# Weight sums of a Winograd feed-forward product: formed by adding transfers instead of by VectorE

## The chip, the cores and the metric

The kernel runs on one core of one Trainium2 chip. The metric is the device time of one execution in microseconds (us); lower is better. Names used below: PE is the matrix engine (TensorE), DVE is VectorE, ACT is ScalarE, POOL is GpSimd, SP is the engine that issues the ordinary transfers.

## The reference, cut to what matters

One encoder block in float32 over 1024 tokens of width 1024: two gated branches (linear attention and windowed attention), an output projection, and a SwiGLU feed-forward layer. The change lies in the first feed-forward product:

```python
h2 = _rms_norm(x, norm_ffn_g[l])
gu = h2 @ w_ffn_in[l]                      # 1024 x 1024 times 1024 x 5632
ff_gate, ff_up = gu[..., :D_FF], gu[..., D_FF:]     # D_FF = 2816 = 22 tiles of 128
x = x + (jax.nn.silu(ff_gate) * ff_up) @ w_ffn_out[l]
```

## The kernel before, in words

Each float32 operand is split into a rounded high part and a low remainder (`wsplit` for weights, L853: ACT writes `wh`, then DVE writes `wl`), and each product is three passes (high-high, high-low, low-high). A `product` (L878) of four 128-row pieces is therefore 12 matmuls of 128x128 by 128x512.

The first feed-forward product uses the Winograd form of Strassen's scheme. For each of the 22 feature tiles f the weights are four blocks of 128x512: A11 and A12 (gate feature tile f, first and second half of the contraction), A21 and A22 (up feature tile f). The activations are four blocks B11, B12, B21, B22 (contraction half by token half), whose own combinations (`combos`, L720) are made once: T1, T2, T3, T4. Seven products per tile replace eight:

- `p11(f)`: A11 with B11, `p21(f)`: A12 with B21 added in the same bank. These give the gate of the first token half.
- `ffn_in(f)`: s1 with T1 (into the bank Z), s2 with T2 (into X), then the products named in `between`, then s3 with T3 (into X), s4 with B22 (into Z), A22 with T4 (into X). Here s1 = A21 + A22, s2 = s1 - A11, s3 = A11 - A21, s4 = A12 - s2, each formed by DVE in `comb` (L873, the addition is L875).

Below, "product 22(f)" is s4 with B22, "T3(f)" is s3 with T3, and so on. Between T2(f) and T3(f) stand one product for f = 0 to 5 (so a tile is six products there) and two for f = 6 to 20 (seven products).

The order of PE is that of the code (a manual schedule for PE alone). The order of DVE, ACT, SP and POOL is chosen by the framework's scheduler when the program is built, and each of these engines then runs its own list strictly in that order: an instruction that waits holds everything behind it. What an instruction waits for are semaphores; in the order shown below, DMASW0 to DMASW7 belong to transfers issued by POOL, DMAHW0 to DMAHW7 to those issued by SP.

Buffers that matter: `wh` and `wl` have five buffers each, so the split of a product can be made when the product five places earlier has ended; `ws` (the sums) has four, `wr` four, `wr2` three. Two reads of the banks free them: `u2` is read from X after T2(f) and before T3(f) overwrites it with its sum, and `c22` is read between T3(f) and A22 with T4. So T3(f) on PE waits for the DVE instruction that makes `u2` (L952 before, L955 after the change).

Of the kernel before, what the change touches and what calls it, by code (L numbers as in the profile page):

```python
# [12 lines left out]
ALU = mybir.AluOpType  # L13
# [8 lines left out]
NFF = 22  # L22
NA = 4
NB = 7
# [5 lines left out]
def body(tc, i, out):  # L30
    nc = tc.nc
    with ExitStack() as root:
# [8 lines left out]
        def nm(s):  # L41
            uid[0] += 1
            return f"{s}_{uid[0]}"

        def mmtile(shape=(P, 512), dt=F32):
            return psm.tile(list(shape), dt, tag="mm", name=nm("mm"))

        def chtile(shape, dt=F32):
            return psc.tile(list(shape), dt, tag="ch", name=nm("ch"))
# [634 lines left out]
        for n in range(2 * KT):  # L684
            g, t = divmod(n, KT)
# [25 lines left out]
        YX = {q: [] for q in ("11", "T1", "T2", "21", "22", "T3", "T4")}  # L711

        def bsplit(pool, tag, src):
            h = pool.tile([P, HT], FR, tag=tag + "h", name=nm(tag + "h"))
            l = pool.tile([P, HT], FR, tag=tag + "l", name=nm(tag + "l"))
            nc.scalar.activation(h, src, AF.Copy)
            nc.vector.tensor_tensor(l, src, h.bitcast(F32), op=ALU.subtract)
            return h, l

        def combos(k, step):  # L720

            b11, b12, b21, b22 = xg[k][0], xg[k][1], xg[k + 4][0], xg[k + 4][1]
            if step == 0:
                YX["11"].append(bsplit(big1, f"b11{k}", b11))
                YX["21"].append(bsplit(big1, f"b21{k}", b21))
            elif step == 1:
                nc.vector.tensor_tensor(b12, b12, b11, op=ALU.subtract)
                YX["T1"].append(bsplit(big2, f"bt1{k}", b12))
                YX["22"].append(bsplit(big2, f"b22{k}", b22))
                nc.vector.tensor_tensor(b22, b22, b12, op=ALU.subtract)  # L730
                YX["T2"].append(bsplit(big2, f"bt2{k}", b22))
                nc.vector.tensor_tensor(b11, b22, b11, op=ALU.subtract)
                nc.vector.tensor_tensor(b21, b21, b22, op=ALU.subtract)
            else:
                YX["T3"].append(bsplit(big3, f"bt3{k}", b11))
                YX["T4"].append(bsplit(big3, f"bt4{k}", b21))
# [116 lines left out]
        def wsplit(src, n):  # L853
            h = wp.tile([P, n], FR, tag="wh", name=nm("wh"), bufs=5)
            l = wp.tile([P, n], FR, tag="wl", name=nm("wl"), bufs=5)
            nc.scalar.activation(h, src, AF.Copy)  # L856
            nc.vector.tensor_tensor(l, src, h.bitcast(F32), op=ALU.subtract)  # L857
            return h, l

        def rload(f, q):  # L860

            if q < 20:
                u = i["w_fi"][f, q - 11]
            else:
                u = i["w_fi"][NFF + f, q - 21]
            if q % 10 == 1:
                t = wp.tile([P, 512], F32, tag="wr", name=nm("wr"), bufs=4)
            else:
                t = wq.tile([P, 512], F32, tag="wr2", name=nm("wr2"), bufs=3)
            nc.sync.dma_start(out=t, in_=u)  # L870
            return t

        def comb(x, y, op):  # L873
            t = wq.tile([P, 512], F32, tag="ws", name=nm("ws"), bufs=4)
            nc.vector.tensor_tensor(t, x, y, op=op)  # L875
            return t

        def product(o, w, x, nk, start, stop):  # L878
            h, l = w
            for kk in range(nk):  # L880
                c = slice(kk * P, (kk + 1) * P)
                nc.tensor.matmul(o, h[:, c], x[kk][0], start=start and kk == 0, stop=False, skip_group_check=True)  # L882
                nc.tensor.matmul(o, h[:, c], x[kk][1], start=False, stop=False, skip_group_check=True)  # L883
                nc.tensor.matmul(o, l[:, c], x[kk][0], start=False, stop=kk == nk - 1, skip_group_check=True)  # L884
# [9 lines left out]
        def ctile(tag):  # L894
            t = x1s.tile([P, HT], F32, tag="xg" + home[tag][turn[tag] % len(home[tag])], name=nm(tag))
            turn[tag] += 1
            return t
# [12 lines left out]
        def put(q, j, k, t):  # L910
            d = scratch(f"{q}{j}_{k}")
            nc.sync.dma_start(out=d, in_=t)
            scr[q, j, k] = d
# [5 lines left out]
        def p11(f):  # L919
            F = feats[f]  # L920
            F.Y = mmtile()
            if f < NB:
                w = wunit(i["w_fi"][f, 0])
            else:
                F.r11 = rload(f, 11)
                w = wsplit(F.r11, 512)
            product(F.Y, w, YX["11"], 4, True, False)
            F.p1 = ctile("a" if f < NA else "p1")
            nc.scalar.copy(F.p1, F.Y)
# [6 lines left out]

        def ffn_in(f, between):
            F = feats[f]
            if f < NB:
                F.r11 = rload(f, 11)  # L940
            F.r12, F.r21, F.r22 = (rload(f, q) for q in (12, 21, 22))
            p1 = F.p1
            Z, X = chtile((P, HT)), mmtile()
            s1 = comb(F.r21, F.r22, ALU.add)
            product(Z, wsplit(s1, 512), YX["T1"], 4, True, False)
            p5 = ctile("p5")
            nc.scalar.copy(p5, Z)
            nc.vector.tensor_tensor(p5, p5, p1, op=ALU.add)
            s2 = comb(s1, F.r11, ALU.subtract)
            product(X, wsplit(s2, 512), YX["T2"], 4, True, False)  # L950
            u2 = ctile("u2")
            nc.vector.tensor_tensor(u2, X, p1, op=ALU.add)  # L952
            for p, g in between:
                p(g)
            s3 = comb(F.r11, F.r21, ALU.subtract)  # L955
            product(X, wsplit(s3, 512), YX["T3"], 4, False, False)
            c22 = ctile("c22")
            nc.vector.tensor_tensor(c22, X, p5, op=ALU.add)
            s4 = comb(F.r12, s2, ALU.subtract)
            product(Z, wsplit(s4, 512), YX["22"], 4, False, True)  # L960
            nc.vector.tensor_tensor(u2, Z, u2, op=ALU.add)
            nc.vector.tensor_tensor(u2, u2, r1, op=ALU.mult)
            nc.scalar.activation(u2, u2, AF.Silu)
            nc.vector.tensor_tensor(u2, u2, r1, op=ALU.mult)
            product(X, wsplit(F.r22, 512), YX["T4"], 4, False, True)
            c21, g0 = ctile("c21"), F.g0
            nc.vector.tensor_tensor(c21, X, p1, op=ALU.add)
            nc.vector.tensor_tensor(c21, c21, g0, op=ALU.mult)
            nc.vector.tensor_tensor(c22, c22, u2, op=ALU.mult)
            put("B1" if f < DK else "B2", 1, f % DK, c21)  # L970
            put("B1" if f < DK else "B2", 2, f % DK, c22)

            if f < DK:
                t1 = hp.tile([P, HT], F32, tag="tx", name=nm("tx"), bufs=4)
                nc.vector.tensor_tensor(t1, c22, c21, op=ALU.subtract)
                put("T", 1, f, t1)
            else:
                b12, t1, t4 = (hp.tile([P, HT], F32, tag="tx", name=nm("tx"), bufs=4) for _ in range(3))
                nc.sync.dma_start(out=b12, in_=scr["B1", 2, f - DK])
                nc.sync.dma_start(out=t1, in_=scr["T", 1, f - DK])  # L980

                def tsum(j, d, x, y):
                    nc.vector.tensor_tensor(d, x, y, op=ALU.subtract)
                    put("T", j, f - DK, d)

                for v in ((2, t1, c22, t1), (3, b12, c22, b12), (4, t4, c21, t1)):
                    if f < NFF - 1:
                        tsum(*v)
                    else:
                        later.append(lambda v=v: tsum(*v))  # L990
# [61 lines left out]
        with tc.manual_schedule(engines={mybir.EngineType.PE}):  # L1052
            for k in range(4):
                combos(k, 0)
# [10 lines left out]
            for k in range(4):  # L1065
                combos(k, 2)
# [5 lines left out]
            for f in range(NFF):  # L1072
                ffn_in(f, between.get(f, [(p21, f), (p11, f + 1)]))
# [11 lines left out]
            def banks(f):  # L1085
                return [f() for _ in range(4)]
# [14 lines left out]
            Z, X = banks(mmtile), banks(lambda: chtile((P, HT)))  # L1101
            fo_product(Z, 11, ("B1", 1), True, True, lambda k: aload(fo1, 11, k), nop, (fo2, 12), (fo2, 21))
            p1 = [ctile("o1") for _ in range(4)]
# [8 lines left out]
            Z = banks(mmtile)  # L1112
            fo_product(Z, 22, ("T", 4), True, True, lambda k: aload(fo3, 22, k), step4)
            c21 = [ctile("o4") for _ in range(4)]
            add4(c21, Z, p1)
            residual4(c21, 1, 0)
            X = banks(lambda: chtile((P, HT)))
# [4 lines left out]
            Z = banks(mmtile)  # L1122
# [89 lines left out]
```

## Time and profile before

| | |
|---|---|
| median of 3 runs | 1688.89 us (1688.65 to 1688.97) |
| span of the profiled execution | 1687.4 us (the median is 1.5 us above it: the time around the first and last instruction) |
| PE / DVE / ACT / POOL busy | 1670.9 / 1181.0 / 869.3 / 0.2 us |
| first feed-forward product | about 1049 to 1469 us of the span, 22 tiles |
| traffic | 245.85 MB in transfers, mean 146 GB/s, all of it issued by SP |

A row of groups reads: line, engine, operation, output<-input, shapes, count, then the busy time in us, the mean of one in ns, and the idle time before it with what ended it. A row of the timeline reads: start, duration, engine, line, operation, output<-input.

### The profile page before, as it was taken

The numbers are of one execution on the slowest core, as the hardware profiler recorded it, in microseconds if no ns is written. First come the engines' busy times: TensorE is split into PE (matmuls) and PEld (weight loads), VectorE is DVE, ScalarE is ACT, GpSimd is POOL, SyncE is SP. The second block draws the span as 40 slices with busy tenths as digits, with TensorE's granted clock in tenths as the row PEclk, the third lists the DMA queues.
The fourth block names the chain that finished last, engine by engine and source line by source line (L and its number), as shares of the span: only waits on it lengthen the run. The fifth ranks groups of instructions, "written<-read, shape, count | busy, mean of one in ns | idle before, by whom it ended". The sixth has DMA issues, their size and how long they took to land.

```text
span 1687.4 us, 23673 instructions
## 1 busy us (share of the span) xinstructions
PE 1670.9 (99%) x7880; PEld 1390.1 (82%) x7880; DVE 1181.0 (70%) x2454; ACT 869.3 (52%) x1939; POOL 0.2 (0%) x4
## 2 busy tenths in 40 slices
PE   8999999999999999999999999999999999999999
PEld 6788888888788888888888888888888888788887
DVE  7767777764578666546674468987778877779755
ACT  7554767776557656544553466533333333354443
POOL 0000000000000000000000000000000000000000
PEclk9999999999999999999999999999999999999999
DMA  6533434444533233247764645344224443496433
GB/s 197 157 113 109 123 126 140 131 141 125 175 121 118 83 100 96 74 150 245 235 213 146 188 129 187 113 134 134 94 88 156 163 143 132 152 333 200 146 100 119
DMA packets 153738, 245.85 MB, mean 146 GB/s; under 512 B 17582, under 2 KB 43054, under 8 KB 153616
## 3 DMA queue, kind: packets, MB, share of 16 engines
q1 hardware_dynamic: 153616, 244.34, 45.6%
q8 instruction: 62, 1.02, 0.3%
q14 instruction: 60, 0.49, 0.1%
HBM read 177.17 MB, written 67.11 MB: 145 GB/s over the span
## 4 chain that ended last, share of the span: by engine, by line
PE 97%; DVE 2%; ACT 1%; DMA 0%; issue 0%; SPq 0%; ACTq 0%; DVEq 0%
PE mm L72 48%; PE ch L72 9%; PE mm L1029 7%; PE mm L884 6%; PE mm L882 6%; PE mm L883 6%; PE ch L1029 5%; PE ch L884 2%; PE ch L882 2%; PE ch L883 2%; PE ch L664 1%; PE ch L490 0%; PE ch L614 0%; PE ch L405 0%; DVE cs L364 0%
## 5 line engine op out<-in xcount | busy, mean ns | idle before, releaser
L66 ACT ACTIVATE wh<-wr 128x512 fp32r<-128x512 f32 (+1 forms) x256 | 160.1, 628 | 173.6 <-PE mm L72 149.5
L68 DVE TENSOR_TENSOR wl<-wr,wh 128x512 fp32r<-128x512 f32 (+1 forms) x256 | 174.9, 687 | 89.0 <-ACT wh L66 82.2
L72 PE MATMUL mm<-xh,wh 128*128 128x512 f32 x512 | 203.3, 397 | 5.9 <-ACT wh L66 5.9
L72 PE MATMUL mm<-xl,wh 128*128 128x512 f32 x512 | 203.4, 397 | 0.0
L72 PE MATMUL mm<-xh,wl 128*128 128x512 f32 x512 | 169.4, 397 | 0.0
L72 PE MATMUL mm<-wh,xh 128*128 128x512 f32 x320 | 126.7, 396 | 1.9 <-DVE st L146 1.2
L72 PE MATMUL mm<-wl,xh 128*128 128x512 f32 x320 | 127.3, 398 | 0.0
L72 PE MATMUL mm<-wh,xl 128*128 128x512 f32 x320 | 126.4, 395 | 0.0
L72 PEld LDWEIGHTS mm<-xh,wh 128*128 128x128 f32 x512 | 96.7, 189 | 22.4 <-ACT wh L66 5.9
L856 ACT ACTIVATE wh<-ws 128x512 fp32r<-128x512 f32 x88 | 55.7, 634 | 115.2 <-PE mm L883 69.3
L72 PEld LDWEIGHTS mm<-xl,wh 128*128 128x128 f32 x512 | 96.7, 189 | 16.9
L72 PEld LDWEIGHTS mm<-xh,wl 128*128 128x128 f32 x512 | 94.9, 189 | 16.7 <-DVE wl L68 0.2
L856 ACT ACTIVATE wh<-a 128x512 fp32r<-128x512 f32 x66 | 41.9, 635 | 90.9 <-PE ch L1029 42.2
L856 ACT ACTIVATE wh<-wr 128x512 fp32r<-128x512 f32 x52 | 33.0, 635 | 91.1 <-issue 49.5
L857 DVE TENSOR_TENSOR wl<-a,wh 128x512 fp32r<-128x512 f32 x66 | 45.5, 690 | 41.8 <-ACT wh L856 41.6
L72 PEld LDWEIGHTS mm<-wh,xh 128*128 128x128 f32 x320 | 60.2, 188 | 14.0 <-DVE st L146 1.6
L1029 PE MATMUL mm<-hh,wh 128*128 128x512 f32 x176 | 69.3, 394 | 1.6 <-ACT hh L1001 1.6
L1029 PE MATMUL mm<-hl,wh 128*128 128x512 f32 x176 | 69.1, 393 | 0.5 <-DVE hl L1002 0.5
L1029 PE MATMUL mm<-hh,wl 128*128 128x512 f32 x176 | 69.2, 393 | 0.1
L647 ACT ACTIVATE p<-p,nm,rs 128x384 f32<-128x384 f32 (+1 forms) x64 | 42.9, 673 | 50.3 <-DVE nm L641 50.3
L72 PEld LDWEIGHTS mm<-wh,xl 128*128 128x128 f32 x320 | 60.2, 188 | 10.4
L857 DVE TENSOR_TENSOR wl<-ws,wh 128x512 fp32r<-128x512 f32 x88 | 60.3, 685 | 11.9 <-ACT wh L856 11.9
(508 smaller groups left out, 4419.8 us busy)
## 6 DMA issues: line engine op xcount, KB each, us to landing
wr<-in_w_fi_dram SPq DMA_DIRECT2D x102, 256.0 KB, 2.9
wr<-in_w_t_dram SPq DMA_DIRECT2D x80, 256.0 KB, 2.8
wr<-in_w_f_dram SPq DMA_DIRECT2D x64, 256.0 KB, 2.7
B<-c SPq DMA_DIRECT2D x44, 256.0 KB, 2.1
T<-tx SPq DMA_DIRECT2D x44, 256.0 KB, 2.4
a<-in_w_fo_dram SPq DMA_DIRECT2D x44, 256.0 KB, 5.3
hr<-T SPq DMA_DIRECT2D x44, 256.0 KB, 2.7
hr<-B SPq DMA_DIRECT2D x33, 256.0 KB, 4.3
```

Of the source, the lines that this page charges most:

```text
L66: nc.scalar.activation(h, raw, AF.Copy)
L68: nc.vector.tensor_tensor(l, raw, h.bitcast(F32), op=ALU.subtract)
L72: nc.tensor.matmul(o, a, b, start=start, stop=stop)
L647: nc.scalar.activation(p[:, h, :w], p[:, h, :w], AF.Exp, bias=nm_[:, h:h + 1], scale=a.rs[:, h:h + 1], accum_out=dn[:, h:h + 1])
L664: nc.tensor.transpose(pt[:, h], a.p[:, h, (kb - a.b0) * P:(kb - a.b0 + 1) * P], ident)
L856: nc.scalar.activation(h, src, AF.Copy)
L857: nc.vector.tensor_tensor(l, src, h.bitcast(F32), op=ALU.subtract)
L882: nc.tensor.matmul(o, h[:, c], x[kk][0], start=start and kk == 0, stop=False, skip_group_check=True)
L883: nc.tensor.matmul(o, h[:, c], x[kk][1], start=False, stop=False, skip_group_check=True)
L884: nc.tensor.matmul(o, l[:, c], x[kk][0], start=False, stop=kk == nk - 1, skip_group_check=True)
L1029: nc.tensor.matmul(ys[m], a[:, c], b, start=f0, stop=f1, skip_group_check=True)
```

## The change

The three two-operand sums that DVE formed, and the fourth that follows from them, are formed by transfers: SP loads one block into a tile, and POOL issues transfers that add further blocks into that tile as they land (`plus`, `wsum`). These transfers only add, so the up rows (A21, A22) are taken with the opposite sign: s1 = A21 + A22, s2 = A21 + A22 + A11, A11 + A21 in place of s3 (in the tile that `p11` has read), and s4 = s2 + A12 (in s2's tile, after T2's split has read it). T3 is negated once in `combos`, and the signs of the reads of X and Z follow. Z is started anew by s4 with B22.

```diff
-                nc.vector.tensor_tensor(b11, b22, b11, op=ALU.subtract)
+                nc.vector.tensor_tensor(b11, b11, b22, op=ALU.subtract)
...
-        def comb(x, y, op):
+        def plus(t, f, q):
+            nc.gpsimd.dma_start(out=t, in_=wsrc(f, q), accum_op=ALU.add)
+
+        def wsum(f, *qs):
             t = wq.tile([P, 512], F32, tag="ws", name=nm("ws"), bufs=4)
-            nc.vector.tensor_tensor(t, x, y, op=op)
+            nc.sync.dma_start(out=t, in_=wsrc(f, qs[0]))
+            for q in qs[1:]:
+                plus(t, f, q)
             return t
...
-            if f < NB:
-                F.r11 = rload(f, 11)
-            F.r12, F.r21, F.r22 = (rload(f, q) for q in (12, 21, 22))
+            r11 = rload(f, 11) if f < NB else F.r11
+            F.r12, r22 = rload(f, 12), rload(f, 22)
             p1 = F.p1
+            plus(r11, f, 21)
+            s1, s2 = wsum(f, 21, 22), wsum(f, 21, 22, 11)
             Z, X = chtile((P, HT)), mmtile()
-            s1 = comb(F.r21, F.r22, ALU.add)
-            product(Z, wsplit(s1, 512), YX["T1"], 4, True, False)
+            product(Z, wsplit(s1, 512), YX["T1"], 4, True, True)
             p5 = ctile("p5")
             nc.scalar.copy(p5, Z)
-            nc.vector.tensor_tensor(p5, p5, p1, op=ALU.add)
-            s2 = comb(s1, F.r11, ALU.subtract)
+            nc.vector.tensor_tensor(p5, p5, p1, op=ALU.subtract)
             product(X, wsplit(s2, 512), YX["T2"], 4, True, False)
+            plus(s2, f, 12)
             u2 = ctile("u2")
-            nc.vector.tensor_tensor(u2, X, p1, op=ALU.add)
+            nc.vector.tensor_tensor(u2, X, p5, op=ALU.add)
             for p, g in between:
                 p(g)
-            s3 = comb(F.r11, F.r21, ALU.subtract)
-            product(X, wsplit(s3, 512), YX["T3"], 4, False, False)
+            product(X, wsplit(r11, 512), YX["T3"], 4, False, False)
...
-            s4 = comb(F.r12, s2, ALU.subtract)
-            product(Z, wsplit(s4, 512), YX["22"], 4, False, True)
-            nc.vector.tensor_tensor(u2, Z, u2, op=ALU.add)
+            product(Z, wsplit(s2, 512), YX["22"], 4, True, True)
+            nc.vector.tensor_tensor(u2, Z, u2, op=ALU.subtract)
```

For f below 7 the load of A12 into `r12` is still made, though nothing reads that tile any more.

PE's list is the same, instruction for instruction. Two places where the other lists differ:

POOL, tiles f = 1 to 3, after the change (before, POOL issues no transfer at all). ws_12456 is s2 of tile 2, ws_12315 is s2 of tile 1, ws_12597 is s2 of tile 3, ws_12594 is s1 of tile 3, wr_12446 and wr_12587 are A11 of tiles 2 and 3:

```order
L872 DMA wr_12446<-in_w_fi_dram 128x512 [waits DMAHW4_49,DMAHW2_49,DMAHW5_49,DMAHW0_49,DVE_49]
L872 DMA ws_12456<-in_w_fi_dram 128x512 [waits DMASW3_49,DMAHW6_49,DMASW0_49,DVE_49]
L872 DMA ws_12456<-in_w_fi_dram 128x512 [waits DMASW3_49]
L872 DMA ws_12315<-in_w_fi_dram 128x512 [waits DMASW5_49,DVE_49]
L872 DMA ws_12594<-in_w_fi_dram 128x512 [waits DMAHW1_49,DMASW6_49]
L872 DMA wr_12587<-in_w_fi_dram 128x512 [waits DMAHW2_49,DMAHW5_49,DMASW7_49,DVE_49]
L872 DMA ws_12597<-in_w_fi_dram 128x512 [waits DMAHW6_49,DMASW5_49,DVE_49]
L872 DMA ws_12597<-in_w_fi_dram 128x512 [waits DMASW1_49,DMASW0_49]
```

Two additions into s2 of tile 2 (A22, then A11, the second waiting for the first to land) now stand ahead of the last addition into s2 of tile 1 (A12). The same order repeats up to tile 12; from tile 13 on the last addition of a tile stands ahead of the second addition of the next.

DVE, from the end of tile 0 to `u2` of tile 1, before the change. ws_12398 is s4 of tile 1, wr_2896_12312 its A22; a_12007 is p1, and u_2906_12355 is the `u2` for which T3(1) waits:

```order
L968 TENSOR_TENSOR c_2891_12294<-c_2891_12294,a_12079 128x512 [waits DVE_49]
L857 TENSOR_TENSOR wl_12401<-ws_12398,wh_12400 128x512 [waits Activation_49]
L975 TENSOR_TENSOR tx_12302<-c_2885_12254,c_2891_12294 128x512 [waits DMAHW0_49,DVE_49]
L857 TENSOR_TENSOR wl_12421<-wr_2896_12312,wh_12420 128x512 [waits PE_49,Activation_49]
L948 TENSOR_TENSOR p_2902_12334<-p_2902_12334,a_12007 128x512 [waits Activation_49]
L875 TENSOR_TENSOR ws_12540<-wr_2924_12450,ws_12479 128x512 [waits DMAHW0_49,DVE_49]
L952 TENSOR_TENSOR u_2906_12355<-mm_12315,a_12007 128x512 [waits PE_49]
```

And the same stretch of DVE after the change:

```order
L969 TENSOR_TENSOR c_2888_12293<-c_2888_12293,a_12079 128x512 [waits DVE_49]
L857 TENSOR_TENSOR wl_12399<-ws_12315,wh_12398 128x512 [waits DMASW5_49,Activation_49]
L976 TENSOR_TENSOR tx_12301<-c_2883_12255,c_2888_12293 128x512 [waits DMAHW7_49,DMAHW4_49,DVE_49]
L857 TENSOR_TENSOR wl_12419<-wr_2892_12309,wh_12418 128x512 [waits PE_49,Activation_49]
L951 TENSOR_TENSOR p_2899_12337<-p_2899_12337,a_12007 128x512 [waits Activation_49]
L955 TENSOR_TENSOR u_2902_12357<-mm_12320,p_2899_12337 128x512 [waits DVE_49,PE_49]
```

The addition L875 is gone from the stretch; the split of product 22(1), `wl_12399`, now waits for an adding transfer (DMASW5), and `u2` stands behind it in the list as before.

More of the change, by code (lines that the diff above doesn't have):

```diff
@@ L858, in wsplit, with wsrc @@
             return h, l
+        def wsrc(f, q):
+            return i["w_fi"][f, q - 11] if q < 20 else i["w_fi"][NFF + f, q - 21]
         def rload(f, q):
[L862 to L865, printed above, removed]
             if q % 10 == 1:
@@ L869, in rload @@
                 t = wq.tile([P, 512], F32, tag="wr2", name=nm("wr2"), bufs=3)
-            nc.sync.dma_start(out=t, in_=u)
+            nc.sync.dma_start(out=t, in_=wsrc(f, q))
             return t
-        def comb(x, y, op):
+        def plus(t, f, q):
+            nc.gpsimd.dma_start(out=t, in_=wsrc(f, q), accum_op=ALU.add)
+        def wsum(f, *qs):
             t = wq.tile([P, 512], F32, tag="ws", name=nm("ws"), bufs=4)
-            nc.vector.tensor_tensor(t, x, y, op=op)
+            nc.sync.dma_start(out=t, in_=wsrc(f, qs[0]))
+            for q in qs[1:]:
+                plus(t, f, q)
             return t
@@ L964, in ffn_in @@
             nc.vector.tensor_tensor(u2, u2, r1, op=ALU.mult)
-            product(X, wsplit(F.r22, 512), YX["T4"], 4, False, True)
+            product(X, wsplit(r22, 512), YX["T4"], 4, False, True)
             c21, g0 = ctile("c21"), F.g0
-            nc.vector.tensor_tensor(c21, X, p1, op=ALU.add)
+            nc.vector.tensor_tensor(c21, X, p1, op=ALU.subtract)
             nc.vector.tensor_tensor(c21, c21, g0, op=ALU.mult)
```

## The prediction, on record before the result was known

> **What bounds the kernel now.** I read the page first, then what PE waited for, then the stretch of the first feed-forward product by windows and groups, then that stretch's timelines.
>
> ```profile
> span 1687.4 us, 23673 instructions
> PE 1670.9 (99%) x7880; PEld 1390.1 (82%) x7880; DVE 1181.0 (70%) x2454; ACT 869.3 (52%) x1939; POOL 0.2 (0%) x4
> ```
>
> PE is busy for 99% of the span, DVE for 70%. The 16.5 us that PE is not busy are the most that any relief of another engine could bring without changing PE's list. The complete list of PE's waits says where they are:
>
> ```profile
> PE mm L72 <- ACT wh L66: 5.9, 1, 5.9
> PE ch L490 <- ACT ob L484: 1.6, 1, 1.6
> PE mm L1029 <- ACT hh L1001: 1.6, 1, 1.6
> PE mm L72 <- DVE st L146: 1.2, 1, 1.2
> PE mm L72 <- DVE st L149: 0.7, 1, 0.7
> PE ch L72 <- DVE rt L96: 0.6, 1, 0.6
> PE mm L1029 <- DVE hl L1002: 0.5, 1, 0.5
> PE ch L72 <- DVE sl L420: 0.3, 1, 0.3
> ```
>
> None is at L882 to L884, the lines of the products that the change feeds. Two, 1.6 and 0.5 us, stand at L1029, the product that follows. The windows say the same of the stage (columns: window, length, busy time and count of PE, PE's weight loads, DVE, ACT, POOL, then granted clock, DMA share, GB/s):
>
> ```profile
> 1086.00:1200.00 114.00, 114.00 (x504) 94.39 (x504) 88.96 (x143) 39.07 (x65) 0.00 (x0) 1.00 0.41 132
> 1280.00:1460.00 180.00, 180.00 (x795) 149.05 (x795) 146.30 (x238) 62.17 (x103) 0.00 (x0) 1.00 0.43 144
> ```
>
> PE is busy for all of both windows at full clock. So in this stage PE is the bound, DVE has 22% of idle time in the first window and 19% in the second, and the DMA engines are free for more than half of the time.
>
> **What the removal is worth.** The additions that go are these:
>
> ```profile
> L875 DVE TENSOR_TENSOR ws<-wr,wr 128x512 f32<-128x512 f32 x44 | 30.2, 687 | 8.2 <-DMA wr<-in_w_fi_dram 4.7 <-issue 3.4
> L875 DVE TENSOR_TENSOR ws<-ws,wr 128x512 f32<-128x512 f32 x22 | 15.2, 691 | 0.6
> L875 DVE TENSOR_TENSOR ws<-wr,ws 128x512 f32<-128x512 f32 x22 | 15.1, 685 | 0.0
> ```
>
> 88 instructions, 30.2 + 15.2 + 15.1 = 60.5 us of DVE. They lie beside a PE that never waits for them, so 60.5 us off DVE are worth nothing on the path. The only place where an earlier DVE could show is the seam into L1029: at most 1.6 + 0.5 = 2.1 us, of which the 1.6 hang on ACT. The sign changes (a subtraction in place of an addition, T3 negated once) exchange instructions one for one: zero.
>
> **What is put in their place.** Each tile gets five adding transfers issued by POOL, and SP loads five blocks (A11, A12 and A22, and the first blocks of s1 and s2) where it loaded four. Most of this is done a tile ahead. The one step with a short way is s4: A12 may be added into s2 only when the split for T2(f) has read s2. I call A_f the time at which this last addition has landed. Three things hang on A_f.
>
> First, PE. In DVE's list `u2` of tile f stands behind the split of product 22(f), which waits for A_f, and T3(f) waits for `u2`. The cover is the distance to T3 in PE's timeline:
>
> ```profile
> 1091.25 0.39 PE L882 MATMUL mm<-b110h,wh 128*128 128x512 f32 x1
> 1093.97 0.39 PE L882 MATMUL mm<-bt30h,wh 128*128 128x512 f32 x1
> 1110.29 0.39 PE L882 MATMUL mm<-bt30h,wh 128*128 128x512 f32 x1
> ```
>
> A product takes 1093.97 - 1091.25 = 2.72 us, and T3(1) and T3(2), the second and third row, are 16.32 us apart: six products. Where seven stand between (into f = 6 and later) it is 7 x 2.72 = 19.05.
>
> Second, the lag from A_f to `u2`:
>
> ```profile
> 1292.56 0.63 ACT L856 ACTIVATE wh<-ws 128x512 fp32r<-128x512 f32 x1 [1.12 <-PE mm L883]
> 1293.23 0.69 DVE L857 TENSOR_TENSOR wl<-ws,wh 128x512 fp32r<-128x512 f32 x1 [0.66 <-ACT wh L856]
> ```
>
> ```profile
> 1066.36 0.69 DVE L857 TENSOR_TENSOR wl<-ws,wh 128x512 fp32r<-128x512 f32 x1
> 1089.02 0.69 DVE L857 TENSOR_TENSOR wl<-ws,wh 128x512 fp32r<-128x512 f32 x1
> 1091.43 0.69 DVE L875 TENSOR_TENSOR ws<-wr,ws 128x512 f32<-128x512 f32 x1
> 1092.03 0.68 DVE L952 TENSOR_TENSOR u<-mm,a 128x512 f32<-128x512 f32 x1
> ```
>
> ACT's `wh` gives 0.66 us, `wl` starts then. From the start of `wl` of 22(1) to the end of `u2` the list takes 1092.03 + 0.68 - 1089.02 = 3.69 us, less the L875 step of 0.60 that goes: 3.09. So T3(f) can't start before A_f + 3.75.
>
> Third, the next tiles. s2 of tile f+2 uses the buffer of s2 of tile f, so SP may load its first block only after `wl` of 22(f), 0.66 + 0.69 = 1.35 after A_f. In POOL's list A22's addition into s2 of tile f+2 waits for that load, A11's addition waits until A22's has landed, and A12's addition into s2 of tile f+1 stands behind both. Let N be the time from issue to landing of a plain load, X that of an adding transfer, D the time POOL needs between two issues. Then A_(f+1) = A_f + L with L = 1.35 + N + 2X + D. This loop doesn't exist before the change, and must turn within 16.32 us (19.05 from f = 6 on). From f = 13 the order on POOL lets A12 pass before A11's addition, L loses an X, and the loop is short.
>
> **Sizes.** No adding transfer, and no transfer of POOL's at all, is in the trace. The nearest rows (KB each, median us from issue to landing) are these of 256 KB:
>
> ```profile
> wr<-in_w_fi_dram SPq DMA_DIRECT2D x102, 256.0 KB, 2.9
> B<-c SPq DMA_DIRECT2D x44, 256.0 KB, 2.1
> hr<-B SPq DMA_DIRECT2D x33, 256.0 KB, 4.3
> a<-in_w_fo_dram SPq DMA_DIRECT2D x44, 256.0 KB, 5.3
> ```
>
> ```profile
> 1067.67 0.33 SPq L870 DMA_DIRECT2D wr<-in_w_fi_dram  x1
> ```
>
> ```profile
> GB/s 197 157 113 109 123 126 140 131 141 125 175 121 118 83 100 96 74 150 245 235 213 146 188 129 187 113 134 134 94 88 156 163 143 132 152 333 200 146 100 119
> ```
>
> The lower end of X is a plain load, 2.9, as if the add were free. An adding transfer reads two operands and writes one: a load and a store one after the other are 2.9 + 2.1 = 5.0. The stage gets busier too: of 132 GB/s in the first window, 8 transfers of 256 KB in 16.32 us (128 GB/s) are the bulk; after the change 9 plain and 5 adding ones, each of the latter counted twice, are 19 x 262144 bytes / 16.32 us = 305 GB/s, near the page's busiest slice, 333 GB/s, in which loads of `a` and `hr` took 5.3 and 4.3. I take N = 4.3 and X = 4.3 + 2.1 = 6.4, the busy load with a store. The upper end of X is two of the slowest loads, 2 x 5.3 = 10.6. N lies between 2.9 and 4.3. D is taken as SP's row, 0.3; POOL's own could be from nothing to a few us (a rival).
>
> **The sum.** A_0 comes after T2(0)'s split, which ended at 1066.36 + 0.69 = 1067.05 and loses two L875 steps (1.20): 1065.85 + 6.4 = 1072.25. Then 1.35, the load 4.3, A22 6.4, the issue 0.3 behind A11's, A12 6.4: A_1 = 1091.0. T3(1) then starts at 1094.75 against 1093.97: 0.8 us late. L = 1.35 + 4.3 + 12.8 + 0.3 = 18.75, 2.43 over the six-product period: T3(2) to T3(5) lose 4 x 2.43 = 9.7. From f = 6 the period of 19.05 holds the loop. Sum 10.5 us, all on PE and nothing given back, since PE has no other wait in the stage. 1687.4 + 10.5 = 1697.9 span; the median of before (1688.89) is 1.5 above its profiled span, so 1699.4.
>
> The sum is steep in X. With N = 4.3 it passes 0.2% (3.4 us, about what a measurement of this kernel can tell from no change) at X = 5.8: L = 17.55, A_1 = 1089.2, 1.0 early, 4 x 1.23 - 1.0 = 3.9. With X = 8.5, half-way to the upper end, A_1 = 1097.3 and T3(1) is 7.1 late, L = 22.95 costs 4 x 6.63 = 26.5 and, over 19.05, 3.9 at each of the seven steps into f = 6 to 12, 27.3: together 60.9, time 1749.8.
>
> **Rivals.**
>
> *Hidden.* With X at 5.0 and N at 2.9 (the quiet rows), L is 14.55, A_1 = 1065.85 + 1.35 + 2.9 + 0.3 + 15 = 1085.4, 4.8 us ahead of need, and no T3 waits: 1688.9. For it: the share of the DMA engines in this stage is only 0.41 now, and the loads there now take 2.9. Against: these loads would share the engines with the adding transfers. It ends where X reaches 5.7. The Trainium skill, "DMA: Bandwidth & Descriptors", section "Anatomy of one DMA — SWDGE (gpsimd) path", fits a transfer issued by GpSimd as 2.0 us plus bytes over 436 GB/s; "Collectives: The Full Stack", section "The bandwidth ceiling: the fold count and why AG ≠ RS ≠ AR", says that an inline add costs no cycles but a second source read. By these an estimate for 256 KB is 2.0 + 2 x 0.6 = 3.2 us, L would be 11.0 and the time 1688.9; no transfer in this trace is of that kind, so the trace neither bears it out nor denies it. Chance 0.34.
>
> *The DMA engines become the bound.* In the second window 144 GB/s at a share of 0.43 are, in 19.05 us, 10.5 transfers of 256 KB and 8.2 us of the engines: 0.78 each. After: 11.5 plain ones, 9.0 us, and 5 adding ones. If an adding one costs them three plain ones, 11.7, a tile needs 20.7 and loses 1.6; over the eleven tiles from f = 11, 18 us: time 1707. It decides from 2.6 plain ones on. Against it: twice is what two reads suggest, 16.8. Chance 0.11.
>
> *POOL itself.* If POOL needs 3.8 us or more to issue a transfer, its five per tile (19) overrun any tile; at 4.5, 22.5 - 19.05 = 3.5 over 21 tiles is 73 us: 1762. POOL has 0.2 us of work now, so nothing shows its speed. Chance 0.03.
>
> *Faster.* The whole seam of 2.1 us gained and nothing lost: 1686.8, inside 0.2%. More would need a PE wait that isn't in the list. Chance of over 0.2% faster 0.04.
>
> That the change doesn't do what it says is no case: the additions are gone from DVE's list.
>
> **Numbers.** The forecast's loop gets 0.48. Slower by over 0.2%: 0.48 + 0.11 + 0.03 = 0.62; within 0.2%: 0.34; faster: 0.04. The range goes from the hidden case with the seam, 1686.8, to X = 8.5, 1750; outside lie X near 10.6 and a slow POOL, about 0.1. The forecast's own range is 1692.5 (X = 5.8, 3.6 to 3.9 us over) to 1750.
>
> **What would show it.** After the change, PE's waits should hold the first matmul of T3 behind DVE's `u`, in tiles 1 to 5 only, about 10 us in all; the split of product 22(f) should end a wait for a transfer on POOL's queue; and the adding transfers should take about 6.4 us from issue to landing. If PE shows no such wait, X was under 5.7 and the hidden case holds. If the waits go on after tile 6, X is above 6.5 or POOL or the DMA engines are the bound: then loads of w_ffn_in would show landings far above 4.3. PE waiting for `wh` or `wl` directly, and not for `u`, would make the lag of 3.75 wrong.

## The result, and the profile after

The changed kernel takes 1701.16 us (median of 4 executions, 1699.44 to 1703.23) against 1688.77 us before (4 executions, 1688.52 to 1688.97): the ratio is 1.0073, 95% interval 1.006 to 1.0087. That is 12.4 us slower; 1699.4 was forecast. The profiled execution took 1701.83 us, with a span of 1700.1 against 1687.4: 12.7 us more. The sum that was forecast was nearly right, but only a third of it was lost where the prediction said.

The head of the page after the change, and POOL's queue from its DMA part (packets, MB, share of 16 engines):

```profile
span 1700.1 us, 23948 instructions
PE 1674.9 (99%) x7880; PEld 1390.9 (82%) x7880; DVE 1129.9 (66%) x2366; ACT 865.8 (51%) x1939; POOL 96.5 (6%) x114
```

```profile
q0 software_dynamic: 15840, 28.84, 10.4%
```

DVE's busy time fell by 51 us, and that bought nothing. (The prediction's 60.5 us adds up the lengths of the 88 additions. In the timeline that it shows, the one at 1091.43 lasts 0.69 us and the next instruction starts after 0.60; at that step 88 of them are an estimated 53 us.) POOL's 110 transfers are a queue of their own that takes 10.4% of the engines' time. From the list of PE's waits after the change, the two largest rows that the list of before doesn't have, and the two of the seam into the next product:

```profile
PE mm L72 <- DVE wl L68: 5.0, 2, 3.1
PE mm L885 <- DVE u L955: 3.0, 3, 1.9
...
PE mm L1030 <- ACT hh L1002: 1.3, 1, 1.3
...
PE mm L1030 <- DVE hl L1003: 0.8, 1, 0.8
```

The second row is the forecast wait: T3, on the `u2` of DVE. The first is new. L72 is the product of the stages before the feed-forward layer, and L68 the split of their weights. Its two waits lie near 850 us, 200 us before the first sum is needed. How late PE is at each T3 shows the parts. First the last T3 that is late, T3(5), before the change; then the starts of T3(1) to T3(5) after it, from PE's timeline:

```profile
1159.25 0.39 PE L882 MATMUL mm<-bt30h,wh 128*128 128x512 f32 x1
```

```profile
1102.20 0.39 PE L885 MATMUL mm<-bt30h,wh 128*128 128x512 f32 x1
...
1118.80 0.47 PE L885 MATMUL mm<-bt30h,wh 128*128 128x512 f32 x1
...
1135.84 0.47 PE L885 MATMUL mm<-bt30h,wh 128*128 128x512 f32 x1 [0.44 <-DVE u L955]
...
1154.31 0.47 PE L885 MATMUL mm<-bt30h,wh 128*128 128x512 f32 x1 [1.87 <-DVE u L955]
...
1171.61 0.47 PE L885 MATMUL mm<-bt30h,wh 128*128 128x512 f32 x1 [0.70 <-DVE u L955]
```

T3(1) stood at 1093.97 before: PE comes to it 8.2 us late. T3(5) is 1171.61 - 1159.25 = 12.4 us late. So 8.2 us were lost before the sums' own stage, 4.1 us in T3(2) to T3(5), and 0.3 us after. Of the 4.1 us, 3.0 are the waits on `u2`; what the other 1.1 are was not followed.

The windows of the output stage (columns as in the prediction), the kernel before first, then after:

```profile
815.00:830.00 15.00, 15.00 (x68) 12.43 (x67) 8.09 (x13) 7.39 (x12) 0.00 (x0) 1.00 0.61 179
830.00:845.00 15.00, 15.00 (x68) 12.43 (x67) 11.62 (x19) 8.75 (x15) 0.00 (x0) 1.00 0.75 243
845.00:860.00 15.00, 15.00 (x67) 12.41 (x67) 12.68 (x21) 7.02 (x13) 0.00 (x0) 1.00 0.74 225
```

```profile
815.00:830.00 15.00, 15.00 (x68) 12.43 (x67) 4.99 (x8) 3.35 (x6) 3.51 (x4) 1.00 1.00 279
830.00:845.00 15.00, 14.88 (x66) 11.96 (x66) 7.31 (x12) 6.17 (x11) 0.86 (x1) 1.00 0.82 229
845.00:860.00 15.00, 9.99 (x37) 7.51 (x36) 13.46 (x23) 9.19 (x17) 0.00 (x0) 0.90 0.70 221
```

Between 830 and 860 us PE starts 103 matmuls where it started 135. The 32 missing ones, at 2.72 us for 12, are 7.2 us: nearly all of the 8.2. The cause stands a window earlier: from 815 to 830 the DMA engines go from a share of 0.61 to 1.00, and DVE and ACT do 8 and 6 instructions where they did 13 and 12. What comes on top are transfers of w_ffn_in for the first tiles, for which buffers are free that early: six additions of POOL for tiles 0 and 1, and ten loads in SP's list from 801 to 824 us where there were three. The DMA issues from 813 to 836 us (count, KB, median us to landing), before and after:

```profile
wr<-in_w_ob_dram SPq DMA_DIRECT2D x9, 256.0 KB, 3.2
ga<-ga SPq DMA_DIRECT2D x5, 256.0 KB, 2.7
```

```profile
wr<-in_w_ob_dram SPq DMA_DIRECT2D x7, 256.0 KB, 6.7
ws<-in_w_fi_dram POOLq DMA_DIRECT2D x6, 256.0 KB, 7.6
ga<-ga SPq DMA_DIRECT2D x4, 256.0 KB, 7.2
ws<-in_w_fi_dram SPq DMA_DIRECT2D x2, 256.0 KB, 7.9
wr<-in_w_fi_dram SPq DMA_DIRECT2D x2, 256.0 KB, 7.5
```

Beside six transfers of POOL, the stage's own weights and gates take over twice as long to land. ACT, DVE and SP fall behind, and PE, after some 20 us of grace, waits for the weights. In the last window, after its wait of 3.1 us, it is granted 0.90 of the clock, which is a part of the 7.2.

The chain that ended last shows how SP falls behind there (start, duration):

```profile
811.34 4.99 DMA wr<-in_w_fi_dram
...
816.35 7.52 DMA wr<-in_w_fi_dram
...
824.83 8.40 DMA ga<-ga
```

The first two rows are loads of A12 of tiles 1 and 2, which nothing reads after the change. Such a tile's buffer is free as soon as the load has landed, so the next load into it stands that early in SP's list and waits there for the landing: the second row starts when the first has ended, and the load of `ga`, which the stage itself needs, is issued only after the second has landed. No run takes these unread loads alone out of the changed kernel; the experiments below show POOL's transfers without these loads, and these loads without POOL's transfers.

### The profile page after: what moved, and what is told of

It reads as the page before. It is cut to its first block, busy times and chain, and to the rows that moved or that the text cites. A ratio compares the mean times of both kernels' runs of the same rounds, so it can differ in the third digit from the quotient of the medians.

```text
span 1700.1 us, 23948 instructions
## 1 busy us (share of the span) xinstructions
PE 1674.9 (99%) x7880; PEld 1390.9 (82%) x7880; DVE 1129.9 (66%) x2366; ACT 865.8 (51%) x1939; POOL 96.5 (6%) x114
## 3 DMA queue, kind: packets, MB, share of 16 engines
q0 software_dynamic: 15840, 28.84, 10.4%
## 4 chain that ended last, share of the span: by engine, by line
PE 86%; DMA 6%; DVE 4%; issue 2%; ACT 1%; POOL 0%; SPq 0%; POOLq 0%; ACTq 0%; DVEq 0%
PE mm L72 42%; PE ch L72 9%; PE mm L1030 7%; PE ch L1030 5%; PE mm L885 5%; PE mm L887 5%; PE mm L886 5%; DMA ws<-in_w_fi_dram 2%; PE ch L885 2%; PE ch L887 2%; PE ch L886 2%; PE ch L664 1%; DMA lo<-o 1%; DMA wr<-in_w_fi_dram 1%; DMA lo<-b 1%
## 5 line engine op out<-in xcount | busy, mean ns | idle before, releaser
L68 DVE TENSOR_TENSOR wl<-wr,wh 128x512 fp32r<-128x512 f32 (+1 forms) x256 | 174.6, 685 | 103.1 <-ACT wh L66 98.4
L72 PE MATMUL mm<-xh,wh 128*128 128x512 f32 x512 | 203.7, 398 | 5.7 <-ACT wh L66 5.7
L72 PE MATMUL mm<-xl,wh 128*128 128x512 f32 x512 | 203.6, 398 | 0.0
L72 PE MATMUL mm<-xh,wl 128*128 128x512 f32 x512 | 169.6, 398 | 0.0
L872 POOL DMA_DIRECT2D ws<-in_w_fi_dram x88 | 77.2, 1086 | 1108.6 <-DMA wr<-in_w_oa_dram 812.8
L72 PE MATMUL mm<-wh,xh 128*128 128x512 f32 x320 | 126.7, 396 | 1.9 <-DVE st L146 1.2
L72 PE MATMUL mm<-wl,xh 128*128 128x512 f32 x320 | 127.3, 398 | 0.0
L72 PE MATMUL mm<-wh,xl 128*128 128x512 f32 x320 | 126.4, 395 | 0.0
L72 PEld LDWEIGHTS mm<-xh,wh 128*128 128x128 f32 x512 | 96.8, 189 | 22.7 <-ACT wh L66 6.1
L72 PEld LDWEIGHTS mm<-xl,wh 128*128 128x128 f32 x512 | 96.8, 189 | 17.0 <-DVE xl L271 0.2
L72 PEld LDWEIGHTS mm<-xh,wl 128*128 128x128 f32 x512 | 94.9, 189 | 16.9 <-DVE wl L68 0.5
L856 ACT ACTIVATE wh<-ws 128x512 fp32r<-128x512 f32 x66 | 41.7, 632 | 115.6 <-PE mm L886 53.3
L856 ACT ACTIVATE wh<-wr 128x512 fp32r<-128x512 f32 x74 | 46.7, 631 | 94.9 <-issue 47.7
L72 PEld LDWEIGHTS mm<-wh,xh 128*128 128x128 f32 x320 | 60.2, 188 | 14.0 <-DVE st L146 1.6
L72 PEld LDWEIGHTS mm<-wh,xl 128*128 128x128 f32 x320 | 60.2, 188 | 10.4
L72 PEld LDWEIGHTS mm<-wl,xh 128*128 128x128 f32 x320 | 60.2, 188 | 10.2
```

What stands on the lines that cost most here:

```text
L68: nc.vector.tensor_tensor(l, raw, h.bitcast(F32), op=ALU.subtract)
L72: nc.tensor.matmul(o, a, b, start=start, stop=stop)
L872: nc.gpsimd.dma_start(out=t, in_=wsrc(f, q), accum_op=ALU.add)
```

## The experiments

Each was timed beside the kernel before, whose median was 1688.52 us for the first four, 1689.16 for the next four and 1688.57 for the last two.

**Which tiles.** Two kernels form a part of the sums by DVE as before the change (with the new signs): the first for f below 2, the second for all others (`dve = f >= 2`).

```diff
-            plus(r11, f, 21)
-            s1, s2 = wsum(f, 21, 22), wsum(f, 21, 22, 11)
+            dve = f < 2
+            if dve:
+                r21 = rload(f, 21)
+                s1, s2 = (wq.tile([P, 512], F32, tag="ws", name=nm("ws"), bufs=4) for _ in range(2))
+                nc.vector.tensor_tensor(s1, r21, r22, op=ALU.add)
+            else:
+                plus(r11, f, 21)
+                s1, s2 = wsum(f, 21, 22), wsum(f, 21, 22, 11)
...
+            if dve:
+                nc.vector.tensor_tensor(s2, s1, r11, op=ALU.add)
...
+            if dve:
+                nc.vector.tensor_tensor(s2, s2, F.r12, op=ALU.add)
```

> The sums of tiles 0 and 1 are formed by DVE, from loads that SP issues, as before the change; from tile 2 on by adding transfers. So no adding transfer runs in the stage around 813 to 835 us. Theory A (most of the loss, 7.2 of the 12.7 us of span, is made there: the transfers of the two prefetched tiles fill the DMA engines and delay the loads of the stage's own products): no wait of PE on L68 near 850, and only what the loop of s2 still costs, 0 to 3.5 us: 1689 to 1693 us. Theory B (the waits near 850 are an accident of that one profiled execution, and the loop of s2 carries the loss in the others): 1698 to 1701 us.

> Only tiles 0 and 1 are formed by adding transfers; from tile 2 on DVE forms the sums. Theory A: the 7.2 us near 850 stay, the waits of T3(3) to T3(5) go (3.5 us): 1695 to 1698 us. Theory B: 1688 to 1691 us.

The first took 1694.10 us (ratio 1.0029, 1.0019 to 1.0039), 5.6 over before; the second 1693.55 (1.0028, 1.0015 to 1.0041), 5.0 over. Their waits, from the first and from the second:

```profile
PE mm L885 <- DVE u L964: 3.7, 3, 1.4
```

```profile
PE mm L72 <- DVE wl L68: 1.9, 1, 1.9
```

Each holds one of the two waits and not the other. So the waits near 850 are no accident of one execution, and neither place carries the loss alone. Together they make 10.6 of the 12.4; the difference is within what single executions scatter (four us among those of the changed kernel). The first came out 1 us above what Theory A allowed: the loop of s2 costs rather 5 than 3.5. The second came out 1.5 us below Theory A's range: the early transfers alone cost rather 5 than 7.2.

**The last addition on DVE.**

```diff
-            plus(s2, f, 12)
...
+            nc.vector.tensor_tensor(s2, s2, F.r12, op=ALU.add)
             product(Z, wsplit(s2, 512), YX["22"], 4, True, True)
```

> As after the change, but the last addition, A12 into s2, is made by DVE from the tile that p21 reads, for all tiles; the other adding transfers stay. That opens the loop of s2. Theory A: the waits on u at T3 go, those near 850 stay: 1695 to 1698 us. Theory B: 1688 to 1691 us.

1693.03 us (1.0023, 1.0013 to 1.0034), 4.5 over before, 2 us below Theory A's range. T3 doesn't wait any more; the other row stays:

```profile
PE mm L72 <- DVE wl L68: 3.5, 2, 3.1
```

**Plain transfers.** `plus` without `accum_op`.

> POOL's 112 transfers are issued with the same waits and in the same order, but as plain loads that overwrite (no sums are formed, so the output is of other numbers). What differs is the add alone. If the add is what makes X long (6.1 us): X falls to between 3 and 4.5, no wait on u at T3, and near 850 less than half of the 7.2 us is left: 1689 to 1692 us. If POOL's path or the longer list of SP is what costs: X stays near 6 and the time at 1698 to 1702 us.

1694.26 us (1.0026, 1.0014 to 1.0039), 5.7 over before and between the two ranges. Of the transfers, of which there are 110 and not 112:

```profile
ws<-in_w_fi_dram POOLq DMA_DIRECT2D x88, 256.0 KB, 3.2
```

```profile
q0 software_dynamic: 8800, 28.84, 5.6%
```

```profile
PE mm L72 <- DVE wl L68: 4.5, 2, 3.1
```

The add is what makes X long: 6.1 us with it, 3.2 without, and at 3.2 no T3 waits, as the prediction's loop says for a short X. Near 850 I was wrong: the waits are nearly as long without the add (4.5 us against 5.0), so in the full stretch even plain transfers on top are too many.

**SP's list or POOL's transfers.** On top of the kernel with the last addition on DVE, tiles 0 and 1 are summed by DVE from the loads that SP issues after the change.

```diff
+            if f < 2:
+                s1, s2 = wsum(f, 21), wsum(f, 21)
+                nc.vector.tensor_tensor(s2, s2, r22, op=ALU.add)
+                nc.vector.tensor_tensor(s2, s2, r11, op=ALU.add)
+                nc.vector.tensor_tensor(r11, r11, s1, op=ALU.add)
+                nc.vector.tensor_tensor(s1, s1, r22, op=ALU.add)
```

> As the kernel in which DVE makes the last addition (so no loop of s2), and in addition tiles 0 and 1 are summed by DVE, but from the loads that SP issues after the change (A21 loaded twice into the two sums, at the same places of SP's list). So SP's list near 800 to 830 us is the changed one, and POOL's six transfers there are gone. If SP's longer list alone delays the stage's own loads: waits on L68 near 850 as before, 1692 to 1694 us. If it is the room that POOL's transfers take on the DMA engines: no such waits, 1688 to 1690 us.

1690.13 us (1.0006, 0.9997 to 1.0014): not to be told from before, and no wait on L68 or `u`. The share from 815 to 830 us is between the two kernels':

```profile
815.00:830.00 15.00, 15.00 (x68) 12.43 (x67) 9.37 (x15) 6.75 (x13) 0.00 (x0) 1.00 0.74 248
```

With four loads more than before at their new places in SP's list nothing is late. The kernel with the last addition on DVE has the same seven loads of w_ffn_in there and POOL's six transfers on top, and waits 3.5 us. So POOL's transfers bring the wait without the unread loads of A12, which neither of these two kernels has. Whether six more loads in SP's own list would do the same was not tried. The 80 additions that POOL still makes later cost about 1 us (0.97, by the interval at most 2.4).

**Cutting the loop by buffers.** s1 goes to a `wr` buffer, so that `ws` holds s2 alone, four deep.

> As after the change, but s1 is loaded into a wr buffer, so that the four ws buffers hold s2 alone: the first block of s2 of tile f+2 needn't wait for the split of product 22(f). That cuts the loop of s2 at its buffer; every adding transfer stays, and POOL makes eight of them in the stage near 815 to 840 us in place of six. Theory A (two separate places, the prefetch near 850 us and the loop of s2): no wait on u at T3, the waits near 850 stay or grow by some: 1692 to 1697 us. Rival (T3 waits because adding transfers are slow as such, or because POOL's list is in order, whatever the buffer): the waits on u stay at 3 to 4 us: 1698 to 1703 us.

1701.89 us (1.0073, 1.006 to 1.0085): Theory A missed, the time is in the rival's range, and T3 still waits (2.9 us). POOL's list shows why (ws_12739 is s2 of tile 4, ws_12315 s2 of tile 1):

```
L872 DMA ws_12739<-in_w_fi_dram 128x512 [waits DMASW6_49,DMAHW6_49,DMASW3_49,DVE_49]
L872 DMA ws_12739<-in_w_fi_dram 128x512 [waits DMASW7_49,DMASW6_49]
L872 DMA ws_12315<-in_w_fi_dram 128x512 [waits DVE_49]
```

s2 of tile 4 takes the buffer of tile 0, and the scheduler again put its two additions ahead of the last one of tile 1. The loop was not cut, only made of other tiles; and near 850 there were eight transfers of POOL, with 5.6 us of waits on L68.

**Holding the first sums back** until DVE has made the statistics of the output stage, alone and with the buffers above:

```diff
+            if f < 2:
+                nc.vector.tensor_copy(t[:, 0:1], rstd[:, 0:1])
             nc.sync.dma_start(out=t, in_=wsrc(f, qs[0]))
```

> All sums by adding transfers as after the change, but the loads of s1 and s2 of tiles 0 and 1 wait for a small copy by DVE that needs the statistics of the output stage (near 986 us), so that POOL's six transfers run there and not near 815 to 835 us, where the DMA engines are full. Theory A: no waits near 850; the loop of s2 costs what it costs, 3.5 to 5.5 us: 1692 to 1694.5 us. Rival (the delay near 850 comes from the other loads of w_ffn_in that stay where they are): 1697 us or more.

> Both cures at once: the first sums held back to the output stage, and the ws buffers for s2 alone. All sums are still made by adding transfers. Theory A: both places are clean, 1688 to 1690 us, the time of the kernel before. If a third cost exists (the DMA engines in the second half of the product, POOL's own time): 1691 us or more, with waits of PE in another place.

1698.11 us (1.0055, 1.0042 to 1.0069) and 1700.95 (1.0075, 1.0063 to 1.0088): both above Theory A's ranges. In the first, the wait near 850 is gone, although six loads of w_ffn_in, unread ones of A12 among them, still stand early in SP's list. But another stands near 1010 us, where the held-back transfers now run (second row), and T3's waits are as long as ever (first row):

```profile
PE mm L887 <- DVE u L957: 3.9, 3, 2.1
PE mm L72 <- ACT mh L809: 1.8, 1, 1.8
```

The trace points to the transfers: from 1000 to 1010 us the DMA engines are at a share of 0.95, against 0.48 before, and a load of `gb`, from which `mh` is made, takes 6.5 us, where the median was 2.8 before. A kernel with DVE's four small copies alone was not run.

The second kernel holds back the s2 of the first four tiles and leaves s1 in the `wr` buffers. T3 waits 5.3 us in it and the stage near 1010 us 3.3 for `mh`. A wait of 1.5 us on L68 also remains near 850, although POOL issues nothing there: the early loads in SP's list, again with unread ones of A12, can cost something by themselves. Its profile is of an execution of 1705.80 us, its slowest.

**POOL's list in the order of the code**, alone and with tiles 0 and 1 by DVE:

```diff
-        with tc.manual_schedule(engines={mybir.EngineType.PE}):
+        with tc.manual_schedule(engines={mybir.EngineType.PE, mybir.EngineType.Pool}):
...
-            plus(r11, f, 21)
             s1, s2 = wsum(f, 21, 22), wsum(f, 21, 22, 11)
+            plus(r11, f, 21)
```

> All sums by adding transfers and the same buffers as after the change, but POOL's list in this stage follows the code, as PE's does: the last addition into s2 of tile f (A12) stands ahead of every addition of tile f+1. (Within a tile, A21's addition into the tile of A11 stands behind those of s1 and s2.) In POOL's list of the kernel with s1 in a wr buffer, the refill of s2 for tile f+3 still stood ahead of the last addition of tile f, so the loop was not cut there. Theory A' (it is the place of the last addition in POOL's list that makes T3 wait): no wait on u at T3 beyond 0.5 us. Near 850 three of POOL's transfers are left in place of six, for 0 to 4 us: 1689 to 1694 us. Rival (adding transfers of 6 us are too slow for the period in any order): waits at T2 or T3 of 3 us and more, 1695 us or more.

> POOL's list in the order of the code as in the kernel before this one, and the sums of tiles 0 and 1 by DVE, so no adding transfer near 815 to 835 us; from tile 2 on all five additions of a tile are transfers. Theory A': neither place costs anything, 1688.5 to 1690.5 us. Rival as before: 1693 us or more, as the kernel with the first two tiles by DVE alone.

1696.58 us (1.0047, 1.0034 to 1.0059) and 1690.41 (1.001, 1.0001 to 1.0019). The first is above the range of Theory A' and in that of its rival; the second is at the upper end of its own. The first kernel's two places, from its list of waits:

```profile
PE mm L72 <- DVE wl L68: 3.1, 1, 3.1
PE mm L885 <- DVE c L960: 2.6, 2, 1.5
```

Three early transfers in place of six still cost one wait of 3.1 us. And T3 waits no more, but A22 with T4 now does, for `c22`. In the second kernel (the profile is of its slowest execution, 1692.96 us) the chain of waits shows a loop again, made of other steps (T2's split, POOL's issues, A22's and A11's additions in series):

```profile
1123.21 6.99 DMA ws<-in_w_fi_dram
...
1130.96 0.71 DVE wl L857
...
1132.49 2.11 POOL ws L872 x2
...
1141.23 6.93 DMA ws<-in_w_fi_dram
```

It turns in 1141.23 + 6.93 - 1123.21 - 6.99 = 17.96 us, over 16.32 too. Beside the kernel with the first two tiles by DVE and the scheduler's POOL list (5.6 over before), the code's order costs 1.8: the new places in POOL's list, that of A12's addition and that of A21's, take away about two thirds of that loss. That the additions in series make the rest is read from this chain and was not tried. No kernel was faster than the one before.

## Why the prediction was right, and where it was not

**The bound and the relief: right.** PE is still busy for 99%, no wait went, and taking DVE down by 51 us changed nothing. The seam into the next product still costs 2.1 us (1.3 and 0.8 in place of 1.6 and 0.5).

**The loop: right in mechanism, close in length, too long in its sum.** The chain of waits after the change runs through it step by step, here from A_2 to A_4 and T3(4) ("issue" after a POOL row is POOL's wait for a landing):

```profile
1108.36 6.23 DMA ws<-in_w_fi_dram
...
1125.23 6.39 DMA ws<-in_w_fi_dram
...
1131.73 0.64 ACT wh L856
...
1132.40 0.70 DVE wl L857
1133.12 3.73 DMA ws<-in_w_fi_dram
...
1137.41 0.86 POOL ws L872
1138.27 4.75 issue
...
1143.07 0.51 POOL ws L872
1143.57 6.53 DMA ws<-in_w_fi_dram
...
1153.47 0.70 DVE u L955
```

A_2, A_3 and A_4 are the ends of the three transfers of 6.23, 6.39 and 6.53 us: 1114.59, 1131.62 and 1150.10. The loop turned in 17.0 and 18.5 us, where 18.75 was forecast: split 1.5 (forecast 1.35), load 3.7 (4.3), A22 6.2 with POOL's half a microsecond (6.4), A12 7.0 with its own (6.7 with D). From A_4 to T3(4) are 1154.31 - 1150.10 = 4.2 us (3.75). X was 6.1 us in the median over the kernel against 6.4, POOL's issue 0.86 against 0.3. The waits are in T3 of tiles 3, 4 and 5, and end at tile 6, as forecast. The sum of 10.5 was too large by 6.4: the loop was faster in its first turns, so that T3(1) wasn't late and T3(2) by 0.3 only, and the excess of 0.7 and 2.2 us a turn began a tile later. A loop that is one part in eight over its period is sensitive to each start and each half microsecond.

**The step that failed: "Most of this is done a tile ahead".** This sentence gave the transfers of tiles 0 and 1 no price and named no cover. They are done not a tile but 220 us ahead, in a stretch whose DMA engines were at 0.61 to 0.75 of their time. That stretch lost 7.2 us of span; the kernel with these transfers alone is 5.0 us over the time of before. Nor did the prediction give a price to the loads of A12 that nothing reads, two of which lie on the chain that ended last there. The page of before had the row that should have stopped me, the DMA tenths in 40 slices of 42 us:

```profile
DMA  6533434444533233247764645344224443496433
```

The 19th and 20th slice, 759 to 844 us, have a 7, more than any other but the one with the loads of `a` (9), and the lists of SP and POOL put the first blocks and their additions there. That the total came out within 1.8 us is the chance of two errors that cancel: 10.5 forecast in one place, 4.1 there and 8.2 elsewhere.

**The rivals.** *Hidden* is refuted as a whole, but the plain transfers show its condition to be right: at X = 3.2 no T3 waits. (Its limit, X = 5.7, goes with the load of 4.3 us; with its own load of 2.9 the loop stays within 16.32 us up to X = 5.9.) The Trainium skill, "DMA: Bandwidth & Descriptors", "Anatomy of one DMA — SWDGE (gpsimd) path", fits a transfer issued by GpSimd as 2.0 us plus bytes over 436 GB/s, an estimate of 2.6 us here. The plain ones of POOL took 2.7 us at the least and 3.2 in the median, so the fit is near for them. The prediction's estimate of 3.2 us for an adding one is about half of the 6.1 that were measured.

The add shows in the engines' time as well: 10.4% of 1700.1 us over 110 transfers are 1.61 us each, and without the add 5.6% of 1693.4 us are 0.86, a ratio of 1.9. The packets changed too, from 80 a transfer to 144 (8800 and 15840 over 110), so this ratio alone doesn't show a second read. But SP's plain transfers of 256 KB also come in 144 packets, and they take the engines an estimated 0.86 us each: before the change, from 813 to 836 us, 2552 packets, 4.64 MB and a share of 66.0%. Nearly twice the time at equal packets agrees with the Trainium skill, "Collectives: The Full Stack", "The bandwidth ceiling: the fold count and why AG ≠ RS ≠ AR", which says of the add in a reduce-scatter that it needs two source reads. The landing took 2.9 us longer, which the engines' time doesn't explain.

*The DMA engines as the bound* of the second half didn't come: PE is busy throughout 1280 to 1460 us at a share of 0.85.

```profile
1280.00:1460.00 180.00, 180.00 (x795) 149.04 (x795) 122.50 (x196) 62.60 (x104) 39.29 (x45) 1.00 0.85 223
```

But it is what happened near 815 us, a place that the rival didn't name. *POOL itself* is refuted by its 0.86 us.

## What to carry to other kernels

Price a transfer where the list issues it, not where its data is used: a prefetch with free buffers runs as early as its queue allows, and there it competes with what that stage waits for. An adding transfer cost 1.9 times the DMA time of a plain one here, and in these lists each addition into a tile waits until the one before has landed, so sums of three or four operands become serial chains, and on an in-order queue the last addition waits behind the first ones of a later tile. Moving work off an engine that nobody waits for was worth nothing here, and its new place had a price of its own.

## What the runs showed of the hardware that I had not expected

```profile
DMA to landing us min/median/max: 3.7/6.1/10.1
```

The landing of 256 KB from POOL went from 3.2 us plain to 6.1 with the add, up to 10.1 (the view of L872: least, median, most), while the engines' time per transfer rose by 0.75 us only; what the other 2 us are, no run tells. (The plain ones also met engines that were less busy, at a share of 0.68 against 0.86 from 1086 to 1200 us.) The issue of one held POOL for 0.86 us with the add and for 0.54 without, in the median. With the engines at a share of 1.00, the landing of plain loads beside them rose from 3.2 to 6.7 us. Yet at a share of 0.85, in the second half of the product, no engine that mattered waited.
